# A forgetting-attention and latent-attention layer: decays ahead of the first head, early weight blocks split tile by tile, and copies and small subtractions given to GpSimd

## The chip, the cores and the metric

The kernel runs on one core of a Trainium2 chip. The metric is the device time of one execution in microseconds. Before the change the median of three runs is 655.59 us (654.94 to 655.67).

## The reference

One layer of an encoder: 1024 frames and 16 meta tokens in front of them, model width 1024. One input projection feeds two groups of eight heads. The FoX heads are causal softmax attention with a forgetting bias, the MLA heads are chunk-causal attention on low-rank latents. Both are gated by a SiLU, joined, projected, normed and added to the input.

```python
h = _rmsnorm(x, norm_pre)
proj = h @ w_in
(fq, fk, fv, f_logit, f_gate, c_q, c_kv, k_r, m_gate) = jnp.split(proj, ...)
log_f = jax.nn.log_sigmoid((f_logit + b_f).astype(jnp.float32))
cum = jnp.cumsum(log_f, axis=1).transpose(0, 2, 1)
# FoX: s = q k / 8 + cum[query] - cum[key], key <= query, softmax, times fv
# MLA: q from c_q, k and v from c_kv, rope on 32 of 96 columns, mask by chunks of 64
y = jnp.concatenate([fox, mla], axis=-1) @ w_out
return x + _rmsnorm(y, norm_post)
```

## The kernel before

Nearly every product is made of float16 pairs: an operand is split into a high and a low part, and three products (high by high, high by low, low by high) are summed in PSUM. Scales that keep the pairs in range come from sums of squares.

**Projection stage (0 to about 137 us).** A loop at L583 goes over token tiles of 128 rows. For tile t it norms and transposes tile t + 1 (`norm`, `turn`; the cast to `xBh` or `xAh` is in `split`, L142), makes the latents and the forget logits (`latents`), the FoX values (`values`) and the MLA values (`latents_V`). Between these, weight blocks for the later stages are loaded to staging buffers with the tag "wr2" (`load_block(..., True)`, four buffers). Four early blocks (`raws_e`) are split to pairs by `block_parts` (L149 on ACT, L150 on DVE) when t is 5. Twelve late blocks are loaded three at a time when t is 5 to 8; each is only squared and summed (`square_block`, L465 on ACT), for its scale. `scale_blocks` turns the sums to scales. Behind the loop, `lu` (L644) is the log of the forget gates.

**Decays.** `decays` (L961) transposes `lu` (L969), copies it to `zt` (L971, L975), sums it along the frames (L976), takes its size (L979, L980, L982, a product cm at L984) and derives from it the factors of the FoX operands, `fox_c` (L997), `fox_qc` and `fox_inv`; it scales `ncum` (L986, L987) and cuts it into three float16 parts (`cparts`, L1005 to L1008), which go through DRAM into rows 64 to 66 of the operand K2 (L1041). It is called from the job of head 0, behind the products of its first chunk.

**FoX heads (about 158 to 400 us).** `fox_proj(h)` makes the operands of head h in three chunks of columns (512, 264, 264): `chan_group` has 24 products (L955 to L957) into one of two PSUM buffers, then ACT copies queries to QS[0:64] and Q2[0:64] (L1047, L1048) and keys to KS[0:64] and KS[64:128] (L1049, L1050), and DVE writes the low parts QS[64:128] and K2[0:64] (L1053, L1054), after which the PSUM buffer is free. The work of head h + 1 and of the gates runs in slices between the four steps of head h.

**A step** (`step`, L873) takes two query tiles: scores on PE (L793, L796), maxima on DVE (L803, L804, L808), exponentials on ACT to `pr` (L816), high parts on ACT to `ph` (L829). One step later DVE writes the low parts (L833) and the low parts of the 16 meta columns (L898), and SP issues a transposing DMA of `ph` to `pT` (L901). Three steps after the scores PE multiplies with the values (L841, L842) and DVE sums the result (L913). `pr` has two buffers, `ph` three (filled with zeros once, L771), `pT` three. MLA heads run the same steps from about 400 to 600 us; the output projection follows.

The program builder takes the source order as a priority and places an instruction on its engine by when its inputs should be there, so that the order on an engine is not that of the source.

## Time and profile before

| | us |
|---|---|
| median of the runs | 655.59 |
| profiled execution, its own time | 651.95 |
| its span, first to last instruction | 650.2 |
| PE busy in the span | 562.1 |
| DVE busy | 501.2 |
| ACT busy | 421.4 |
| GpSimd (POOL) busy | 148.7 |

The profiled execution is one run of the program; its own time is a little under the median of the runs. Busy times are unions over the span, and those of PE are modelled ends of pipelined matmuls. An idle time in brackets is that of the engine just before the instruction, with the instruction or DMA whose end released it; where several were waited for, it names the one that came last by the profile. PEclk is the share of 2.4 GHz that TensorE was granted.

### The profile page before, as it was taken

The page shows a single profiled execution, that of the slowest core. Times are in us where ns is not written, and L with a number is a line of the kernel's source. Part 1 is how long each engine was busy: PE and PEld are TensorE (multiplying, and loading weights), DVE is VectorE, ACT ScalarE, POOL GpSimd, SP SyncE. Part 2 cuts the span into 40 slices and gives each one's busy share as a digit, 9 for nine tenths or more (in the row PEclk, how much of TensorE's full clock was granted, in tenths as well). Part 3 has the DMA queues.
Part 4 walks back from the last instruction along what each step waited for, and adds up shares of the span by engine and source line. Part 5 has one row for each costly group of instructions (what it writes and reads, how often), then busy time and mean ns, then how long its engine had stood idle before and what let it go on. Part 6 is the DMA issues. An engine that isn't in the chain of part 4 may idle for free.

```text
span 650.2 us, 11363 instructions
## 1 busy us (share of the span) xinstructions
PE 562.1 (86%) x4100; PEld 362.4 (56%) x4100; DVE 501.2 (77%) x1048; ACT 421.4 (65%) x855; POOL 148.7 (23%) x179
## 2 busy tenths in 40 slices
PE   1999598992899999899999986978989989987994
PEld 1445254551556565656566543555756756666784
DVE  4787965458677978787887988779998887995667
ACT  6686757643777686767687737567866776646332
POOL 2233333274000101010010331003102202262462
PEclk9999798995999999999999988998999999999998
DMA  9945569935175968495969667599999799799963
GB/s 305 231 118 127 113 121 241 225 85 150 42 152 124 187 133 174 105 222 111 231 115 204 143 157 145 112 229 218 162 227 178 164 211 187 158 227 211 313 233 122
DMA packets 277944, 112.36 MB, mean 173 GB/s; under 512 B 235312, under 2 KB 265008, under 8 KB 277888
## 3 DMA queue, kind: packets, MB, share of 16 engines
q1 hardware_dynamic: 277888, 111.64, 76.1%
q8 instruction: 32, 0.52, 0.3%
q14 instruction: 24, 0.20, 0.1%
HBM read 52.05 MB, written 17.63 MB: 107 GB/s over the span
## 4 chain that ended last, share of the span: by engine, by line
DVE 33%; PE 30%; ACT 19%; DMA 8%; issue 7%; POOL 1%; SPq 0%; DVEq 0%; ACTq 0%; POOLq 0%
ACT pr L816 8%; DVE ph L833 7%; DVE nb L803 5%; ACT ph L829 4%; PE s L793 4%; DMA pT<-ph 3%; DVE nb L804 3%; PE psg L955 2%; DMA wr<-in_w_in 2%; PE psg L956 2%; PE psg L957 2%; PE avs L842 2%; DVE nbs L808 2%; DVE st L1054 1%; PE psf L1251 1%
## 5 line engine op out<-in xcount | busy, mean ns | idle before, releaser
L833 DVE TENSOR_TENSOR ph<-pr,ph 128x896 f16<-128x896 f32 (+7 forms) x128 | 104.2, 822 | 38.2 <-ACT ph L829 37.5
L816 ACT ACTIVATE pr<-s,nbs,fox_inv 128x144 f32<-128x144 f32 (+8 forms) x72 | 56.1, 784 | 56.3 <-DVE nbs L808 54.0
L793 PE MATMUL s<-st,st 128*128 128x348 f16 (+6 forms) x434 | 77.3, 307 | 14.5 <-DVE st L1053 8.2
L816 ACT ACTIVATE pr<-s,nbs,ism 128x144 f32<-128x144 f32 (+8 forms) x72 | 56.1, 785 | 42.6 <-DVE nbs L808 19.1
L842 PE MATMUL avs<-Vt,pT 128*128 128x128 f16 x704 | 69.7, 222 | 12.9 <-DMA pT<-ph 6.6
L793 PEld LDWEIGHTS <-st 128*128 128x128 f16 x560 | 50.9, 98 | 48.8 <-issue 14.2
L829 ACT CAST ph<-pr 128x912 f16<-128x912 f32 (+6 forms) x112 | 77.6, 737 | 0.3
L803 DVE TENSOR_REDUCE nb<-s 128x1 f32<-128x344 f32 (+4 forms) x80 | 68.2, 857 | 7.6 <-PE s L796 6.5
L842 PEld LDWEIGHTS <-pT 128*128 128x128 f16 x704 | 59.3, 99 | 14.7 <-DMA pT<-ph 12.9
L841 PE MATMUL avs<-Vt,pT 128*128 128x64 f16 x576 | 61.7, 194 | 0.0
L841 PEld LDWEIGHTS <-pT 128*128 128x128 f16 x576 | 51.1, 99 | 4.3 <-issue 3.7
L955 PEld LDWEIGHTS <-wp 128*128 128x128 f16 x320 | 31.8, 99 | 34.5 <-DVE st L1054 11.2
L850 POOL TENSOR_TENSOR onat<-onat,rs 128x512 f32<-128x512 f32 x8 | 8.8, 1103 | 164.4 <-DVE onat L913 141.3
L956 PEld LDWEIGHTS <-wp 128*128 128x128 f16 x320 | 31.7, 99 | 26.3 <-issue 5.6
L957 PEld LDWEIGHTS <-wp 128*128 128x128 f16 x320 | 31.8, 99 | 25.8 <-issue 1.7
L955 PE MATMUL psq<-xAh,wp 128*128 128x264 f16 x128 | 36.2, 283 | 3.0 <-DVE st L1054 2.6
L956 PE MATMUL psq<-xAl,wp 128*128 128x264 f16 x128 | 36.1, 282 | 0.0
L957 PE MATMUL psq<-xAh,wp 128*128 128x264 f16 x128 | 36.1, 282 | 0.0
L804 DVE TENSOR_REDUCE nb<-s 128x1 f32<-128x144 f32 (+1 forms) x64 | 31.9, 498 | 3.6 <-PE s L796 3.2
L145 POOL TENSOR_TENSOR ogl<-ogr,ogh 128x512 fp32r<-128x512 f32 (+1 forms) x16 | 19.8, 1238 | 46.8 <-ACT ogh L142 46.8
L955 PE MATMUL psg<-xAh,wp 128*128 128x512 f16 x64 | 24.3, 380 | 7.1 <-DVE st L1054 7.1
L145 POOL TENSOR_TENSOR st<-qt,st 128x512 f16<-128x512 f32 x8 | 10.2, 1274 | 81.2 <-ACT st L142 81.2
(367 smaller groups left out, 1574.3 us busy)
## 6 DMA issues: line engine op xcount, KB each, us to landing
wr<-in_w_in SPq DMA_DIRECT2D x20, 512.0 KB, 5.4
wr<-in_w_in SPq DMA_DIRECT2D x26, 256.0 KB, 3.9
wor<-in_w_out SPq DMA_DIRECT2D x8, 512.0 KB, 4.9
xt<-in_x SPq DMA_DIRECT2D x7, 512.0 KB, 5.1
og_d<-og SPq DMA_DIRECT2D x14, 256.0 KB
y_d<-ys SPq DMA_DIRECT2D x12, 256.0 KB, 2.2
y<-y_d SPq DMA_DIRECT2D x6, 512.0 KB
xr<-in_x SPq DMA_DIRECT2D x6, 512.0 KB, 4.8
```

The costliest lines, as they stand in the source:

```text
L145: lo_eng.tensor_tensor(lo, raw, hi.bitcast(F32) if hi.dtype == F32R else hi, ALU.subtract)
L793: T.matmul(o, sta[:, i * P : (i + 1) * P], mov[:, k0 : k0 + w], start=q == 0, stop=q == len(passes) - 1 and not last)
L803: V.tensor_reduce(nb[:, k : k + 1], part, AX.X, ALU.max, negate=True)
L804: V.tensor_reduce(nb[:, 1:2], parts_b[0], AX.X, ALU.max, negate=True)
L816: A.activation(pr[:, c0:c1], part, AF.Exp, bias=nb, scale=inv, accum_out=sums[:, c : c + 1])
L829: A.copy(ph[:, 112 : 112 + W], pr)
L833: V.tensor_tensor(lo, pr[:, NM:W], ph[:, P : P + W - NM], ALU.subtract)
L841: T.matmul(avf[:, 0:HD], lo[:, j - 1, :], Vt[:, j, vh, 0], start=False, stop=False)
L842: T.matmul(avf, hi[:, j, :], Vt[:, j, vh].rearrange("p t d -> p (t d)"), start=j == 0, stop=j == n)
L955: T.matmul(ps[:, 0:n], hi[:, c, :], xT(0, c, c0, n), start=c == 0, stop=False)
L956: T.matmul(ps[:, 0:n], hi[:, c, :], xT(1, c, c0, n), start=False, stop=False)
L957: T.matmul(ps[:, 0:n], lo[:, c, :], xT(0, c, c0, n), start=False, stop=c == NC - 1)
```

## The change

It has five parts. The staging tag "wr2" gets a fifth buffer. Each early block is split in its own tile, t = 4 to 7, and the twelve late blocks are loaded in tiles 5 to 7 (3, 4 and 5). The zeroing of `ph` covers the 96 columns of two blocks that nothing else writes. `decays` is called before the job of head 0, and in it the scaling of `ncum` comes behind `fox_inv`. In FoX, Q2[0:64] and KS[64:128] are copied by GpSimd from QS[0:64] and KS[0:64], where ACT read PSUM a second time. The low parts of the meta columns (L898) are made by GpSimd, in all 64 steps.

```diff
--- before.py
+++ after.py
@@ -244,7 +244,7 @@
     def load_w(k, cols):
 
         pl, tag = ((fw, "wr"), (xa, "wr2"))[k % 2]
-        raw = pl.tile([P, 2, 512], F32, name="wraw", tag=tag, bufs=3 if k % 2 == 0 else 4)
+        raw = pl.tile([P, 2, 512], F32, name="wraw", tag=tag, bufs=3 if k % 2 == 0 else 5)
         o = 0
         for c0, n in cols:
             SY.dma_start(raw[:, :, o : o + n], wv[:, 2 * (k % 4) : 2 * (k % 4) + 2, c0 : c0 + n],
@@ -451,7 +451,7 @@
     def load_block(block, staged=False):
         kind, k = block
         segs = {"q": ((COL_FQ + k * HD, HD), (COL_FK + k * HD, HD)), "f": ((COL_FG + k * P, P),), "m": ((COL_MG + k * P, P),)}[kind]
-        pl, tag, bufs = (xa, "wr2", 4) if staged else (fw, "wr", 3)
+        pl, tag, bufs = (xa, "wr2", 5) if staged else (fw, "wr", 3)
         raw = pl.tile([P, NC, P], F32, name="wr", tag=tag, bufs=bufs)
         o = 0
         for c0, n in segs:
@@ -599,13 +599,13 @@
         for b, raw in raws_l:
             square_block(b, raw)
         raws_l = []
+        if t < NT:
+            b, raw = raws_e[t - 4]
+            early[b] = block_parts(b, raw)
+            if t > 4:
+                raws_l = [(b, load_block(b, True)) for b in [late_blocks.popleft() for _ in range((3, 4, 5)[t - 5])]]
         if t == 5:
-            for b, raw in raws_e:
-                early[b] = block_parts(b, raw)
             wkr0 = load_ukv(0)
-        if t >= 5:
-            raws_l = [(late_blocks.popleft(), None) for _ in range(3)]
-            raws_l = [(b, load_block(b, True)) for b, _ in raws_l]
         if t == 6:
             sums = xa.tile([P, 4], BF16, name="usums")
             for c in range(2):
@@ -625,8 +625,6 @@
             turn(t + 1)
 
 
-    for b, raw in raws_l:
-        square_block(b, raw)
     latents_T(NT)
     z = xa.tile(FN, F32, name="z")
     V.tensor_tensor(z, fnat, bf.unsqueeze(1).to_broadcast(FN), ALU.add)
@@ -768,7 +766,7 @@
     NPH = 3
     phs = [at.tile([P, NBLK * P], F16, name=f"ph{k}", tag=f"ph{k}", bufs=1) for k in range(NPH)]
     for ph in phs:
-        G.memset(ph, 0.0)
+        G.memset(ph.rearrange("p (b k) -> p b k", k=P)[:, 0 : NT + 3 : NT + 2, 0:96], 0.0)
 
     WT = 344
 
@@ -895,7 +893,7 @@
                 low(i, p, h, l)
             ph, n1 = prev["ph"].rearrange("p (b k) -> p b k", k=P), prev["prw"].rearrange("p (b k) -> p b k", k=NM)
             w0 = 1 + 8 * (prev["t"][0] + 1)
-            V.tensor_tensor(ph[:, 0 : B0 + 1 : B0, 96:112], n1[:, 0 : w0 + 1 : w0, :],
+            G.tensor_tensor(ph[:, 0 : B0 + 1 : B0, 96:112], n1[:, 0 : w0 + 1 : w0, :],
                             ph[:, 0 : B0 + 1 : B0, 112:128], ALU.subtract)
             prev["pT"] = at.tile([P, NBLK * P], F16, name="pT", tag="pT", bufs=3).rearrange("p (b k) -> p b k", k=P)
             SY.dma_start_transpose(prev["pT"], prev["ph"])
@@ -983,9 +981,6 @@
         cm = ps_s.tile([P, 2, 512], F32, name="cm", tag="s2")[:, 0, 0:H]
         T.matmul(cm, ones8, dg, start=True, stop=True)
 
-        V.tensor_scalar(cmh[:, 1:2].bitcast(I32), cmh[:, 0:1].bitcast(I32), -1.0, float(268 << 23), ALU.mult, ALU.add)
-        V.tensor_scalar(ncum, ncum, cmh[:, 1:2], None, ALU.mult)
-
 
         e = at.tile([P, 5, H], F32, name="fe", tag="fe")
         cme, emax, ie, ex, cmx = (e[:, k, :] for k in range(5))
@@ -999,6 +994,9 @@
         V.tensor_tensor(fox_qc, cmx, ex, ALU.mult)
         V.reciprocal(ie, ex)
         V.scalar_tensor_tensor(fox_inv, ie, 0.125, ie, ALU.mult, ALU.mult)
+
+        V.tensor_scalar(cmh[:, 1:2].bitcast(I32), cmh[:, 0:1].bitcast(I32), -1.0, float(268 << 23), ALU.mult, ALU.add)
+        V.tensor_scalar(ncum, ncum, cmh[:, 1:2], None, ALU.mult)
         cparts = []
         for k in range(NCUM):
             cparts.append(at.tile([P, NBLK * P], F16, name=f"cp{k}", tag="pT", bufs=3)[0:H, 0:L])
@@ -1035,8 +1033,6 @@
                 ps = product("psq")
                 yield from chan_group(ps, w, c0, n)
                 if k == 0:
-                    if h == 0:
-                        decays()
                     G.tensor_copy(Q2[64 : 64 + n3, 0:S], fox_qc[64 : 64 + n3, h : h + 1].to_broadcast([n3, S]))
                     SY.dma_start(K2[64 : 64 + n3, :], cum_d[:, h, :])
                 q0 = max(c0, NM)
@@ -1045,13 +1041,13 @@
                 pk = ps[64:128, 0:n]
                 ks = slice(c0, c0 + n)
                 A.activation(QS[0:64, qs], pq, AF.Copy, scale=cq)
-                A.activation(Q2[0:64, qs], pq, AF.Copy, scale=cq)
                 A.activation(KS[0:64, ks], pk, AF.Copy, scale=ckk)
-                A.activation(KS[64:128, ks], pk, AF.Copy, scale=ckk)
+                G.tensor_copy(Q2[0:64, qs], QS[0:64, qs])
+                G.tensor_copy(KS[64:128, ks], KS[0:64, ks])
 
                 def evac(pq=pq, pk=pk, qs=qs, ks=ks):
                     V.scalar_tensor_tensor(QS[64:128, qs], pq, cq, QS[0:64, qs], ALU.mult, ALU.subtract)
-                    V.scalar_tensor_tensor(K2[0:64, ks], pk, ckk, KS[64:128, ks], ALU.mult, ALU.subtract)
+                    V.scalar_tensor_tensor(K2[0:64, ks], pk, ckk, KS[0:64, ks], ALU.mult, ALU.subtract)
                 evacuate_later(evac)
                 yield n / 400.0
         return 10.4, gen(), load_w(("q", h), w)
@@ -1095,6 +1091,7 @@
         for g in GATES[h]:
             add_job(h, *gate_job(*g))
 
+    decays()
     add_job(-1, *fox_proj(0))
     fox_jobs(0)
     work(-1, 3.0)
```

## Rows read from the trace of the kernel before

**Rows 1.** Windows: stretch, length, busy PE, PEld, DVE, ACT, POOL, clock, DMA share, GB/s

```profile
74.00:84.30 10.30, 6.10 (x17) 2.49 (x18) 8.98 (x18) 7.12 (x13) 5.19 (x9) 0.50 0.72 146
149.20:162.80 13.60, 4.03 (x18) 2.61 (x19) 10.54 (x24) 5.08 (x10) 4.02 (x3) 0.50 0.41 110
164.00:347.00 183.00, 174.20 (x1394) 109.78 (x1392) 146.42 (x272) 135.00 (x256) 12.31 (x11) 1.00 0.73 147
430.00:600.00 170.00, 148.18 (x1267) 107.59 (x1264) 145.18 (x298) 116.70 (x244) 41.10 (x28) 0.98 0.93 198
```

**Rows 2.** Timeline of PE: start, duration, instruction, [idle before, releaser]

```profile
75.96 0.53 PE L304 MATMUL ps<-w1h,xBh 128*128 128x424 f16 x1 [4.68 <-ACT xBh L142]
79.09 0.90 PE L420 MATMUL pl<-ident,nt 128*128 128x128 f32 x3 [2.23 <-DVE nt L397]
...
150.25 0.16 PE L984 MATMUL cm<-dg,ones 8*128 8x8 bf16 x1 [3.49 <-POOL ph L771]
158.62 0.47 PE L793 MATMUL s<-st,st 128*128 128x344 f16 x1 [8.20 <-DVE st L1053]
```

**Rows 3.** timeline of all engines from 136 to 160 us, the decays

```profile
136.38 0.23 DVE L644 SCALAR_TENSOR_TENSOR lu<-z,lu 128x72 f32<-128x72 f32 x1
...
137.15 0.38 PE L969 MATMUL pf<-ident,lu 128*8 128x128 f32 x2
...
142.70 0.82 PE L969 MATMUL pf<-ident,lu 128*8 128x128 f32 x6
...
143.44 0.16 ACT L971 COPY zt<-pf 8x16 f32<-8x16 f32 x1 [4.67 <-DMA vm_d<-vm]
...
143.56 6.58 POOL L771 MEMSET ph<- 128x2560 f16 x3 [0.63 <-DMA wqr<-in_w_uq]
...
144.69 2.31 DVE L976 TENSOR_TENSOR_SCAN ncum<-ones8f,zt 8x1040 f32<-8x1040 f32 x1 [6.57 <-ACT zt L975]
...
147.66 2.49 DVE L982 TENSOR_SCALAR dg<-ident,cmh 8x8 bf16<-8x8 f32 x1
...
154.89 0.21 DVE L997 SCALAR_TENSOR_TENSOR fox_c<-fe,isx,bisc 128x8 f32<-128x8 f32 x1
...
155.14 0.68 ACT L1047 ACTIVATE st<-psq,fox_c 64x512 f16<-64x512 f32 x1 [9.36 <-DVE fox_c L997]
...
158.59 0.75 DVE L1054 SCALAR_TENSOR_TENSOR st<-psq,fox_c,st 64x512 f16<-64x512 f32 x1
```

**Rows 4.** timeline, the early blocks at 70 us; ACT later in the projection

```profile
70.79 1.28 DVE L150 SCALAR_TENSOR_TENSOR wp<-wr,bsc,wp 128x1024 f16<-128x1024 f32 x1
70.85 2.17 ACT L149 ACTIVATE wp<-wr,bsc 128x1024 f16<-128x1024 f32 x2
...
75.32 1.07 ACT L142 CAST xBh<-pt 128x512 f16<-128x512 f32 x2
...
104.46 1.06 ACT L465 ACTIVATE junkb<-wr 128x1024 bf16<-128x1024 f32 x1 [2.50 <-DMA wr<-in_w_in]
```

**Rows 5.** groups of ACT from 164 to 347 us: count, busy us, mean ns, idle before

```profile
L1050 ACT ACTIVATE st<-psq,fox_c 64x264 f16<-64x264 f32 (+1 forms) x19 | 10.3, 541 | 0.2
```

**Rows 6.** who PE waited for: us in total, times, longest us

```profile
PE psg L955 <- DVE st L1054: 7.1, 5, 1.6
```

**Rows 7.** timeline of DVE before PE's wait at 211 us

```profile
209.12 0.97 DVE L803 TENSOR_REDUCE nb<-s 128x1 f32<-128x784 f32 x1
...
210.10 0.47 DVE L1053 SCALAR_TENSOR_TENSOR st<-psq,fox_c,st 64x248 f16<-64x248 f32 x1
```

**Rows 8.** groups of DVE: count, busy us, mean ns, idle before

```profile
L898 DVE TENSOR_TENSOR ph<-pr,ph 128x32 f16<-128x32 f32 x64 | 18.4, 287 | 0.1
```

**Rows 9.** timeline, POOL and DVE at 247.5 us

```profile
247.54 1.08 POOL L1040 CAST st<-fox_qc 3x1024 f16<-3x1024 f32 x1 [2.24 <-PE s L796]
...
247.64 1.01 DVE L898 TENSOR_TENSOR ph<-pr,ph 128x32 f16<-128x32 f32 x1
```

**Rows 10.** groups of POOL by form: count, busy us, mean ns, idle before

```profile
L402 POOL TENSOR_TENSOR t<-kr,rnat 128x32 f32<-128x32 f32 x9 | 3.4, 376 | 53.1 <-DVE kr L400 53.1
```

## The prediction, made before the changed kernel was seen

> **What bounds the kernel now.** I read the busy shares by stretch first, then the places where PE idles and who ended that idling, then the instructions around the two worst of them. TensorE sets the pace: it is busy 174.2 of 183.0 us in the FoX heads and 148.2 of 170.0 us in the MLA heads, where DVE with 145.2 us is nearly as full [rows 1]. So time is won where PE waits. Two places stand out. Near 76 us, in the projection stage, PE waits 4.68 us and then 2.23 us, and the whole stretch 74.0 to 84.3 runs at a granted clock of 0.50, that is 1.2 instead of 2.4 GHz [rows 1, 2]. Between the projection and head 0 it waits 3.49 and 8.20 us, with only the 0.16 us product cm between, and the clock falls to 0.50 again until 162.8 us [rows 1, 2]. The rest is small: 7.1 us in five waits for L1054 in FoX [rows 6], scattered waits in MLA.
>
> The instructions of an engine do not stand in the order of the source: two of the transposes of `decays` (L969) ran at 137.15 us, ahead of the first product of the job that calls it, six at 142.70 behind it [rows 3]. A moved line therefore changes a priority, and only shifts what was not put there anyway.
>
> **Part 1, decays first, small memsets, half of the ACT copies at head 0.** `lu` is done at 136.61 (136.38 + 0.23), yet the bulk of the transposes comes 6 us later; ACT had nothing to do for the 4.67 us before 143.44 [rows 3]. From there the chain is serial: copies 1.25 us (143.44 to 144.69), scan 2.31, two small steps 0.66, dg 2.49, then 4.85 us from cm at 150.25 to the end of `fox_c` at 155.10, because DVE does pieces of `ncum` and `cparts` in between [rows 2, 3]. dg is an 8x8 operation and ends at 150.15, within 0.01 us of the end of the memsets (143.56 + 6.58 = 150.14); an operation as small as L997 takes 0.21 us [rows 3]. So the large memsets cost 2.3 us here. With `decays` ahead: nine transposes at 0.14 us (six took 0.82) from 137.15 to 138.4, ACT free at 138.77, copies until 140.0, scan until 142.3, small steps until 143.0, dg until 143.2, and the same 4.85 us to `fox_c` at 148.1 instead of 155.10. I keep the 4.85 us: `ncum` now stands behind `fox_inv` in the source, but L1005 and L1008 stood there before and were put into the chain all the same. That is 7.0 us.
>
> Behind `fox_c`, the first chunk took 4.20 us to leave its PSUM buffer (L1047 at 155.14 to the end of L1054 at 159.34): four ACT copies of 0.68 us one after the other and then two DVE operations of 0.75 us [rows 3]. With two ACT copies, and L1053 beside the second of them, L1054 ends 0.68 + 0.68 + 0.75 = 2.1 us after the start, which gives another 2.1 us. PE goes on at about 150.2 instead of 159.34, 9.1 us earlier. At the lower clock PE did 4.03 us of work between 149.2 and 162.8 [rows 1], 2.0 us of which come back if the shorter idle time (146.8 to 150.2) does not bring the clock down; I take 0.9. Sum: 10.0 us. Bounds: at least 2.3 + 2.1 = 4.4 us if nothing moves, at most 159.34 - 146.8 + 2.0 = 14.5 us, since the first two chunks keep PE busy until 146.8 (150.25 - 3.49) [rows 2]. The low end needs the 4.67 us that ACT idled to stay unused, so I stay above the middle. The three stores of `cparts` and the load of K2's rows on SP move with the chain; scores need them only in their second pass, behind the third chunk, so I cost them at nothing; if chunk 3 no longer covers them, what shows is part of the 4.85 us that DVE spends on `cparts` and the chain.
>
> **Part 2, early blocks one per tile, five staging buffers.** At 70 us four splits come in a row; two ACT halves take 2.17 us, a DVE half 1.28 us, and the cast of `xBh`, for which PE waits, comes at 75.32 [rows 2, 4]. The scale of the blocks exists only just before, so the first two splits (tiles 4 and 5) stay at this place and two go to tiles 6 and 7. That takes 2.2 us from ACT and 2.6 us from DVE ahead of PE: the wait of 4.68 us falls to 2.5, that of 2.23 us to about nothing, together 4.4 us, and part of the 3.05 us that 6.10 us of work lost at the low clock [rows 1]; I take 1.0 of it. The two splits moved cost what ACT and DVE had free there, which I put at nothing while PE is the slower; if that cover is gone they cost 2.4 us each on DVE or ACT. The twelve late blocks are now loaded in three tiles (3, 4, 5) instead of four (3 each), on the same SP queue as the x tiles and stores; ACT waited 2.50 us for such a block at 104.46 [rows 4], and its casts stand behind that. For this I take 0.4 off. Sum: 5.0 us, between 0 and 9.9 (4.68 + 2.23 + 3.05).
>
> **Part 3, second places copied by GpSimd.** In FoX ACT loses two of four copies per chunk, 0.54 us each [rows 5]. What PE waits for is L1054 on DVE, and in the repeated case at 211 us DVE came to L1053 straight from L803 with no idle time [rows 7]: a faster ACT alone does not move it. Of the 7.1 us [rows 6] I take 1.5; the bounds are 0 and 7.1. The copies themselves: no copy of this shape is in the trace; a cast of 1024 columns took 1.08 us [rows 9], so 512 columns take 0.54 and 250 to 264 take 0.27, 2.2 us per head and 17.6 us in all. Only the scores of the next head need them, and the projection that makes them ends while the present head still runs, so I let PE wait for none. But GpSimd holds up DVE: L898, whose mean is 0.29 us, took 1.01 us and ended with the cast beside it [rows 8, 9]. If all 17.6 us fell on a DVE that PE waits for, they would cost 17.6 us; PE-bound FoX hides nearly all, I take 0.5 loss. The Trainium skill ("SBUF — State Buffer", Who interferes with whom) says that a DVE instruction with two SBUF inputs contends with a GpSimd instruction that reads SBUF, and that the second one blocks fully; the pair at 247.54 agrees. By the same page an instruction that only writes blocks merely the two-port modes, and the memset beside the scan and dg fits: the scan ran, dg waited.
>
> **Part 4, meta low parts to GpSimd.** DVE loses 64 operations, 18.4 us [rows 8]. On GpSimd a subtraction of 128x32 took 0.38 us [rows 10], 24.1 us for 64. Its inputs are there as soon as the low parts can start, so it runs beside L833, which also reads twice from SBUF, and may hold it up as long. The transposing DMA then waits for GpSimd and DVE; queued behind a GpSimd operation, it comes later, with three steps of slack. Half of either lies in MLA: at best 9.2 us gained there, at worst 12.0 - 9.2 = 2.8 us lost; PE waits in only part of the steps, so I take 0.5 gain.
>
> **Sum.** 10.0 + 5.0 + 1.5 - 0.5 + 0.5 = 16.5 us. The profiled execution took 651.95 us around a span of 650.2 us; that gives 635.45. The median of the runs, 655.59, is 3.64 above it, so 639.1, rounded to 639.0.
>
> **The rivals.** Moved lines land where they were: only the memset's 2.3 us, 2.1 us of shorter evacuation and 1.0 us elsewhere remain, 650.2 us. For it: two transposes were already early [rows 3]. Against: the other seven were not, and ACT stood idle.
>
> Loads too dense: each of the three tiles in which ACT waits for late blocks adds some 2.5 us of it [rows 4], which eats part 2: 644.1 us. For it speaks DMA 0.72 busy near 74 us [rows 1], against it that the fifth buffer lets the first load start earlier.
>
> All waits go: 14.5 + 9.9 + 4, 627.2 us.
>
> The lock on the other side: copies and metas hold DVE up in full, 17.6 + 24.1 - 18.4 = 23.3 us, against 15.0 us from parts 1 and 2: 663.9 us. It decides once more than 65% of the 23.3 us lies in front of PE. For it: the 1.01 us pair, and DVE 85% busy in MLA; against it: FoX is PE-bound [rows 1], and the 18.4 us that DVE gives up stand in it already. The Trainium skill ("Perfetto Trace Analysis", Optimizing Scalar/DVE Operations) warns that moving work between these two engines might not help for this reason; no run here has shown it yet for such small operations.
>
> **How the numbers follow.** Forecast (630 to 648) 50%, moved lines stay 13%, dense loads 15%, all waits go 15%, lock 7%. The range 625 to 650 leaves out the lock, half of the first rival and a part of the third. Faster by over 0.2% (1.3 us, about what a measurement of this kernel can tell from no change): 91%; within: 3%; slower: 6%.
>
> **What would show it.** Right: all L969 before the first L955 of head 0, the scan starting near 140 us after the same `lu`, dg near 0.2 us, PE's idle time before head 0 at 3 to 5 us instead of 11.7, the two waits near 76 us under 3 us together, and FoX and MLA as long as before within 3 us. Wrong: if L969 still runs behind the first chunk, if ACT waits for `wr` loads behind 100 us, or if L833's mean in MLA rises by more than 0.1 us and the heads become longer.

## The result, and the profile of the changed kernel

The changed kernel takes 636.52 us in the median of 4 runs (636.23 to 638.45), the kernel before beside it 655.27: a ratio of 0.972, 95% interval 0.970 to 0.974. In a later set of runs the two took 635.06 and 655.27, ratio 0.970 (0.967 to 0.973). The forecast was 639.0, range 625 to 650. The profiled execution took 636.23 us around a span of 634.4; its granted clock is 0.977 in the mean, before 0.964.

The lines of the changed kernel carry numbers two to five lower: L967 to L974 are the transposes, the copies into `zt` and the scan (before L969 to L976), L980 is dg (before L982), L992 `fox_c` (before L997), L791 the scores (before L793). L1036 is GpSimd's cast of `fox_qc`, L1043 and L1044 are ScalarE's copies, L1045 and L1046 GpSimd's, L1049 and L1050 the low parts (before L1053 and L1054), L896 the meta low parts (before L898). ACT is ScalarE, DVE VectorE, POOL GpSimd, PE TensorE.

I cut the two spans at six events that both traces have; head 7 ends with its last reduction, at 422.3 us before and at 406.9 after. The numbers are differences of start and end times, in us:

| stretch | before | after | gain |
|---|---|---|---|
| start to the first matmul | 9.93 | 11.06 | -1.13 |
| first matmul to `lu` | 126.68 | 118.09 | 8.59 |
| `lu` to the end of `fox_c` | 18.49 | 17.01 | 1.48 |
| `fox_c` to the first score | 3.52 | 3.90 | -0.38 |
| first score to the end of head 7 (FoX) | 263.66 | 256.86 | 6.80 |
| heads 8 to 15 (MLA) | 186.85 | 186.30 | 0.55 |
| rest | 41.06 | 41.23 | -0.17 |

So nearly everything came from the first stage and the FoX heads, and the decays (third and fourth row), on which most of the forecast rested, gave 1.1 us. The first row is no effect: in the profiles of all runs here the first matmul starts between 9.4 and 11.1 us, in two of the changed kernel itself at 11.06 and 10.57.

The windows of the changed kernel that answer to the first two of [rows 1] (stretch, length, busy time of PE, PEld, DVE, ACT, POOL, clock, DMA share, GB/s):

```profile
76.40:79.90 3.50, 3.50 (x12) 1.57 (x10) 3.46 (x10) 3.47 (x10) 1.28 (x7) 0.51 0.71 148
144.70:155.00 10.30, 4.94 (x23) 3.38 (x24) 6.30 (x16) 3.00 (x6) 5.22 (x6) 0.50 0.51 126
```

The half-clock stretch near 76 us has shrunk from 10.2 us to 3.4, the one around the first score from 13.7 to 10.2. PE's waits that answer to [rows 2], on its timeline (start, duration, instruction, idle before it and releaser):

```profile
73.66 0.35 PE L304 MATMUL ps<-w1h,xBh 128*128 128x424 f16 x1 [2.33 <-ACT xBh L142]
76.08 0.35 PE L306 MATMUL ps<-w1h,xBl 128*128 128x424 f16 x1 [1.89 <-DVE xBl L145]
...
141.28 0.16 PE L982 MATMUL cm<-dg,ones 8*128 8x8 bf16 x1 [1.34 <-issue]
...
150.06 0.45 PE L791 MATMUL s<-st,st 128*128 128x344 f16 x1 [7.94 <-POOL st L1046]
```

The 4.68 us have become 2.33, the 2.23 us 1.89 and the 3.49 us 1.34, but the wait for the first score is 7.94 us where it was 8.20, and GpSimd's copy of KS now ends it. The decays between, on the timeline of all engines, to be laid beside [rows 3]:

```profile
128.92 0.23 DVE L642 SCALAR_TENSOR_TENSOR lu<-z,lu 128x72 f32<-128x72 f32 x1
...
130.46 1.04 PE L967 MATMUL pf<-ident,lu 128*8 128x128 f32 x8
...
131.46 0.62 ACT L351 CAST vm<-vs 128x512 f16<-128x512 f32 x1
...
133.16 1.16 POOL L352 TENSOR_TENSOR vm<-vs,vm 128x512 f16<-128x512 f32 x1
...
134.34 0.36 SPq L438 DMA_DIRECT2D vm_d<-vm  x1
...
136.74 0.16 ACT L969 COPY zt<-pf 8x16 f32<-8x16 f32 x1 [4.66 <-DMA vm_d<-vm]
...
136.86 0.66 POOL L769 MEMSET ph<- 128x192 f16 x3 [0.63 <-DMA wqr<-in_w_uq]
...
137.99 2.31 DVE L974 TENSOR_TENSOR_SCAN ncum<-ones8f,zt 8x1040 f32<-8x1040 f32 x1 [6.57 <-DMA wqr<-in_w_uq]
...
140.97 0.22 DVE L980 TENSOR_SCALAR dg<-ident,cmh 8x8 bf16<-8x8 f32 x1
```

Eight of nine transposes are done by 131.5 us, much as forecast. But ACT, free at 132.08, begins the copies only at 136.74, 7.59 us after the end of `lu` (129.15); before it was 6.83 (143.44 - 136.61). The wait that ends with the store of `vm` is there in both kernels: 4.67 us in [rows 3], 4.66 here, where the store lands at 136.64 us.

### The profile page after: what moved, and what is told of

Same layout as the page of the kernel before. It is cut to its first block, busy times and chain, and to the rows that moved or that the text cites. A ratio compares the mean times of both kernels' runs of the same rounds, so it can differ in the third digit from the quotient of the medians.

```text
span 634.4 us, 11456 instructions
## 1 busy us (share of the span) xinstructions
PE 555.5 (88%) x4100; PEld 361.3 (57%) x4100; DVE 485.2 (76%) x984; ACT 397.2 (63%) x807; POOL 217.0 (34%) x291
## 4 chain that ended last, share of the span: by engine, by line
PE 37%; DVE 27%; ACT 15%; DMA 10%; issue 8%; POOL 1%; SPq 1%; DVEq 0%; ACTq 0%; POOLq 0%
ACT pr L814 7%; DVE ph L831 5%; DVE nb L801 4%; PE s L791 4%; ACT ph L827 4%; DMA pT<-ph 4%; PE psg L953 3%; PE psg L954 3%; PE psg L955 3%; DMA wr<-in_w_in 3%; PE avs L840 2%; DVE nb L802 2%; PE psq L953 2%; PE psf L1247 2%; PE psf L1246 2%
## 5 line engine op out<-in xcount | busy, mean ns | idle before, releaser
L831 DVE TENSOR_TENSOR ph<-pr,ph 128x128 f16<-128x128 f32 (+7 forms) x128 | 109.4, 863 | 38.6 <-ACT ph L827 37.2
L896 POOL TENSOR_TENSOR ph<-pr,ph 128x32 f16<-128x32 f32 x64 | 48.3, 755 | 203.3 <-ACT ph L827 106.7
L791 PE MATMUL s<-st,st 128*128 128x348 f16 (+6 forms) x434 | 77.4, 308 | 16.0 <-POOL st L1046 8.2
L791 PEld LDWEIGHTS <-st 128*128 128x128 f16 x560 | 51.0, 98 | 49.6 <-issue 14.4
L801 DVE TENSOR_REDUCE nb<-s 128x1 f32<-128x344 f32 (+4 forms) x80 | 68.2, 857 | 11.4 <-PE s L794 8.2
L150 DVE SCALAR_TENSOR_TENSOR wp<-wr,bsc,wp 128x1024 f16<-128x1024 f32 x21 | 28.2, 1342 | 0.0
L953 PE MATMUL psg<-xBh,wp 128*128 128x512 f16 x64 | 25.0, 391 | 2.9 <-DVE og L859 2.2
```

What stands on the lines that cost most here:

```text
L791: T.matmul(o, sta[:, i * P : (i + 1) * P], mov[:, k0 : k0 + w], start=q == 0, stop=q == len(passes) - 1 and not last)
L801: V.tensor_reduce(nb[:, k : k + 1], part, AX.X, ALU.max, negate=True)
L831: V.tensor_tensor(lo, pr[:, NM:W], ph[:, P : P + W - NM], ALU.subtract)
L896: G.tensor_tensor(ph[:, 0 : B0 + 1 : B0, 96:112], n1[:, 0 : w0 + 1 : w0, :], ph[:, 0 : B0 + 1 : B0, 112:128], ALU.subtract)
L953: T.matmul(ps[:, 0:n], hi[:, c, :], xT(0, c, c0, n), start=c == 0, stop=False)
```

## The experiments

Each is the changed kernel with one edit, unless it says otherwise. Ratios are to the kernel before, run beside it; the changed kernel's are 0.972 and 0.970. The runs came in three sets, in which the median of the kernel before was 654.51, 655.66 and 655.27 us, so I read nothing into 1 us between sets. Lengths of stretches come from one profiled execution of each kernel.

### The decays: order of the calls, or a wait on a store

The memory map of the built program suggests why the store is the releaser. A pool is a region of memory from which tiles are taken; when it is closed, a later pool may be laid over it. `zt` and `ncum` are tiles of the pool `at`, which covers part of the closed pool `xs`. The reading to be tested is that whoever first writes a tile of `at` waits for everything still outstanding on all of `xs`. Its last user is the store of `vm`, though `vm` itself lies above the end of `at` and `zt` shares no byte with `xs`. One run takes the reason of the wait away, one puts the order of the calls back.

```
+    xv, xv_st = pool("xv", side="right")
     xs, xs_st = pool("xs", bufs=2, side="right")
...
-        lat = xs.tile([P, 2, 4, P], F16, name="lat", tag="lat", bufs=3)
+        lat = xv.tile([P, 2, 4, P], F16, name="lat", tag="lat", bufs=3)
...
-        vm = xs.tile([P, H, 2, HD], F16, name="vm", tag="vm", bufs=1)
+        vm = xv.tile([P, H, 2, HD], F16, name="vm", tag="vm", bufs=1)
...
     xs_st.close()
+    xv_st.close()
```

> The changed kernel with one move: the tiles lat and vm, which stores to HBM read late, get a pool of their own that lies above the memory of the pool at. The memory map, the tiles and every instruction stay the same. Theory A (in the decays the copies into zt, the first tiles of the pool at, wait for everything that was still outstanding on the closed pool xs below it, last of all the store of vm, and that is the 4.66 us of ScalarE before the copies at 136.74 us in the profile of the changed kernel): the copies begin within 0.5 us of the end of the last Vt/vm cast at 132.08, fox_c comes 4 to 5 us earlier, and the time is 3.5 to 5.5 us below the changed kernel's 636.5, 631 to 633. Rival B (ScalarE had nothing else to do there, as my prediction read the row of before; the copies are late for another reason, or the chain after fox_c takes up the gain): the time stays within 1 us of 636.5.

Measured: 634.47 us, ratio 0.968 (0.965 to 0.972). Its timeline (line numbers are one or two higher here):

```profile
130.65 0.23 DVE L643 SCALAR_TENSOR_TENSOR lu<-z,lu 128x72 f32<-128x72 f32 x1
133.06 0.16 ACT L971 COPY zt<-pf 8x16 f32<-8x16 f32 x1
...
134.78 2.32 DVE L976 TENSOR_TENSOR_SCAN ncum<-ones8f,zt 8x1040 f32<-8x1040 f32 x1 [1.63 <-ACT zt L975]
...
143.55 0.21 DVE L994 SCALAR_TENSOR_TENSOR fox_c<-fe,isx,bisc 128x8 f32<-128x8 f32 x1
...
147.25 0.47 PE L793 MATMUL s<-st,st 128*128 128x344 f16 x1 [3.98 <-DVE st L1051]
```

The copies come 2.2 us after `lu` and not 7.6, with no wait before them, and ahead of the last store of `vm`, which is issued only at 138.07. The memsets of `ph`, tiles of `at` too, now run at 126.61, before `lu`. `fox_c` ends 12.87 us after `lu` (17.01 in the changed kernel), the first score starts 16.37 after it (20.91), and PE's wait for it is 3.98 us (7.94). So the wait is theory A's, and in the changed kernel it held the first score up by 4.5 us. The time fits neither theory: the median fell by 2.0 us against the first set of the changed kernel and by 0.6 against the later one. At the end of head 0, 3.4 of the 4.5 us are left (70.4 us after `lu`, 73.8 in the changed kernel); in the profiled execution, the slowest of the four, the first stage then took 119.92 us with 6.8 us at half clock (118.09 with 3.4) and the MLA heads 187.15 (186.30).

```
                 if k == 0:
+                    if h == 0:
+                        decays()
...
-    decays()
     add_job(-1, *fox_proj(0))
```

> The changed kernel with the call of decays() put back to where it was, inside the projection of head 0 (the reordered lines inside decays and all other parts of the change stay). Theory A (the order was never what made the copies late, the wait on the store of vm was): the time rises by no more than 2 us, to 636 to 638.5. Rival B (my prediction: the copies were late because they came behind the projection): it rises by about 7 us, to 643.5.

Measured: 635.50 us, ratio 0.970 (0.967 to 0.973): no change, theory A. Its timeline shows that even with six transposes behind the first chunk again the copies begin behind the same wait:

```profile
128.00 0.23 DVE L642 SCALAR_TENSOR_TENSOR lu<-z,lu 128x72 f32<-128x72 f32 x1
...
135.09 0.82 PE L967 MATMUL pf<-ident,lu 128*8 128x128 f32 x6
...
135.82 0.16 ACT L969 COPY zt<-pf 8x16 f32<-8x16 f32 x1 [4.67 <-DMA vm_d<-vm]
```

`lu` to the end of `fox_c` takes 17.01 us in both. In the decays ACT, DVE and POOL run the same instructions in the same order with the call at either place; only PE's order changes.

This shows that the order is worth nothing while the wait stands, and no more than that. The six transposes run from 6.9 to 7.7 us after the end of `lu` here, and the copies start 7.6 after it: the order alone would have held all but the first of the copies up to nearly the same moment as the store. So in the kernel before two hold-ups of almost equal length stood side by side ([rows 3]: transposes from 142.70, copies at 143.44), and the 4.5 us of the run with the pool are those of taking away both. Taking away the late order alone brought nothing. Taking away the wait alone, with the call at its old place, was not run; from these rows I estimate a gain of about 0.3 us.

### The memsets

```
-        G.memset(ph.rearrange("p (b k) -> p b k", k=P)[:, 0 : NT + 3 : NT + 2, 0:96], 0.0)
+        G.memset(ph, 0.0)
```

> The changed kernel with the three memsets of the whole ph tiles again. Theory A (my prediction: dg was held to 2.49 us until the third memset ended, and that stands on the path to fox_c): dg takes about 2 us again where the memsets lie beside it, fox_c comes 1.5 to 2.5 us later after lu, the time rises by 1.5 to 2.5 us, to 637.5 to 639. Rival B (the wait on the store of vm now puts the memsets beside the copies into zt and the scan, and what they hold up there is the scan alone, or nothing, since the next wait behind fox_c, for GpSimd's copies, takes it up): within 0.7 us of 636.

Measured: 636.95 us, ratio 0.973 (0.969 to 0.977). The hold-up of dg is back exactly as in [rows 3]:

```profile
136.58 6.58 POOL L769 MEMSET ph<- 128x2560 f16 x3 [0.62 <-DMA wqr<-in_w_uq]
...
140.70 2.49 DVE L980 TENSOR_SCALAR dg<-ident,cmh 8x8 bf16<-8x8 f32 x1
143.28 0.16 PE L982 MATMUL cm<-dg,ones 8*128 8x8 bf16 x1 [3.61 <-POOL ph L769]
```

`fox_c` ends 19.23 us after `lu`, 2.22 later than in the changed kernel: theory A's size. In the time only 0.4 to 1.9 us of it show, less than theory A's range for it. Head 0 ends 2.8 us later after `lu`, and heads 1 to 7 then take 202.3 us and not 204.0: the half-clock stretch of 3.4 us that lies at 387 us in head 7 of the changed kernel lies at 366 us here. Whether that 1.6 us belongs to the later start or to chance stays open.

### The first stage: the split, or the fifth buffer

Part 2 is two edits: the split of the early blocks, with the loads of late blocks that go with it, and the fifth buffer of the staging ring. Three runs take them apart: the split alone put back, the ring alone put back, and the kernel before with nothing but the ring.

```
-        if t < NT:
-            b, raw = raws_e[t - 4]
-            early[b] = block_parts(b, raw)
...
         if t == 5:
+            for b, raw in raws_e:
+                early[b] = block_parts(b, raw)
...
+            raws_l = [(late_blocks.popleft(), None) for _ in range(3)]
...
```

> The changed kernel with the early blocks split all at token tile 5 again and the late blocks loaded three a tile, the last three squared behind the loop (the ring keeps its five buffers). Theory A (the split one a tile is the whole of the 7.5 us by which the first stage ends earlier, lu at 129.15 and not at 136.61): the time rises by 6.5 to 8.5 us, to 643 to 645, and the half-clock stretch of 10 us near 74 us is back. Rival B (my prediction: worth 5.0 us; the rest came with the fifth buffer, which stays here, or with the run): it rises by 4 to 5.5 us, to 640.5 to 642.

Measured: 637.57 us, ratio 0.972 (0.968 to 0.977): 1 to 2.5 us above the changed kernel, and both theories missed. First matmul to `lu` took 119.41 us.

```
-        raw = pl.tile([P, 2, 512], F32, name="wraw", tag=tag, bufs=3 if k % 2 == 0 else 5)
+        raw = pl.tile([P, 2, 512], F32, name="wraw", tag=tag, bufs=3 if k % 2 == 0 else 4)
...
-        pl, tag, bufs = (xa, "wr2", 5) if staged else (fw, "wr", 3)
+        pl, tag, bufs = (xa, "wr2", 4) if staged else (fw, "wr", 3)
```

> The changed kernel with the staging ring at four buffers, as before; the split one a tile and the loads of 3, 4 and 5 late blocks stay. With the split put back and five buffers kept, lu ended at 130.24 us, 6.4 us earlier than before and only 1.1 later than with the whole change. Theory A (most of the gain of the first stage is the fifth buffer's: it lets the loads of late blocks be issued while the early ones still stand in the ring, so that ScalarE squares late blocks from 55 us on and the queue behind those loads moves up): here lu ends at 133 to 136 us and the time rises by 4 to 6 us, to 639.5 to 642. Rival B (either one alone brings most of it: the two parts mend the same wait, TensorE's 4.68 us before 75.96 in the kernel before): lu ends by 131 and the time stays within 2 us of 636.

Measured: 641.79 us, ratio 0.981 (0.976 to 0.985), `lu` at 134.25 us: theory A in both. The reverse of that diff, applied to the kernel before:

> The kernel before with nothing but a fifth buffer in the staging ring. Theory A (in the first stage the fifth buffer is nearly the whole gain: with it and the old split, lu came 119.4 us after the first matmul, with both 118.1, with the split alone 124.9, before 126.7): here lu comes 119 to 120.5 us after the first matmul and the time is 5 to 7.5 us below before, 648 to 650.5. Rival B (the decays and head 0 take up part of it, or the early end needs the other loads of the change): 651 to 655.

Measured: 646.87 us, ratio 0.988 (0.985 to 0.991), first matmul to `lu` 119.63 us: theory A in the stage, and a time still below its range. Against the profiled execution of before the gain is 5.2 us, against the medians 8.4. So of the 8.59 us of this stage the fifth buffer alone brings 7.05 (126.68 to 119.63), the split alone 1.78 (to 124.90). Two executions of one program differ by up to 1.5 us in this stage (last section), so the 1.78 are hardly clear of that, and the 7.05 are. PE's wait shows the same, with the split and four buffers and then with the old split and five:

```profile
74.22 0.35 PE L304 MATMUL ps<-w1h,xBh 128*128 128x424 f16 x1 [4.68 <-ACT xBh L142]
```

```profile
73.78 0.50 PE L304 MATMUL ps<-w1h,xBh 128*128 128x424 f16 x1 [2.25 <-ACT xBh L142]
```

What the buffer does is seen on ACT and DVE of the kernel before with five buffers:

```profile
55.15 1.06 ACT L465 ACTIVATE junkb<-wr 128x1024 bf16<-128x1024 f32 x1
...
60.94 1.06 ACT L465 ACTIVATE junkb<-wr 128x1024 bf16<-128x1024 f32 x1 [2.31 <-DMA wr<-in_w_in]
...
67.01 0.17 DVE L161 TENSOR_SCALAR bsc<-mb 128x4 int32<-128x4 int32 x1
...
67.33 1.28 DVE L328 SCALAR_TENSOR_TENSOR xt<-xt,rx,gB 128x1024 f32<-128x1024 f32 x1
67.41 1.15 ACT L149 ACTIVATE wp<-wr,bsc 128x1024 f16<-128x1024 f32 x1
```

Two late blocks are loaded early enough to be squared (L465) at 55 and 61 us, where ACT has room; in the kernel before the first late square comes at 76.33. And the order on DVE has changed: the scale of the blocks (L161) stands ahead of the normalisation of an x tile (L328), where before it stood behind it:

```profile
68.01 1.28 DVE L328 SCALAR_TENSOR_TENSOR xt<-xt,rx,gB 128x1024 f32<-128x1024 f32 x1
...
69.40 0.17 DVE L161 TENSOR_SCALAR bsc<-mb 128x4 int32<-128x4 int32 x1
...
69.61 1.15 ACT L149 ACTIVATE wp<-wr,bsc 128x1024 f16<-128x1024 f32 x1 [1.80 <-DVE bsc L161]
```

So ACT's first split starts 2.2 us earlier without a wait, and with it all that follows up to the cast of `xBh`, with the four splits still in one row. Which of the two, earlier squares or the order on DVE, is worth how much was not separated.

### FoX: two copies and a subtraction on GpSimd

```
-                G.tensor_copy(Q2[0:64, qs], QS[0:64, qs])
-                G.tensor_copy(KS[64:128, ks], KS[0:64, ks])
+                A.activation(Q2[0:64, qs], pq, AF.Copy, scale=cq)
+                A.activation(KS[64:128, ks], pk, AF.Copy, scale=ckk)
```

> The changed kernel with the second places of the FoX operands (Q2 rows 0-63, KS rows 64-127) written by ScalarE from PSUM again and not copied by GpSimd. Theory A (the growth of the gain through the FoX heads, from 10.7 us at the end of head 0 to 15.4 us at the end of head 7, is this part's: 0.67 us a head): the time rises by 4 to 6 us, to 640.5 to 642.5; the PE waits in heads 1 to 7 grow by as much. Rival B (my prediction: worth 1.0 us in all, and the growth comes from the other parts through the order of the work): it rises by 0.5 to 1.5 us, to 637 to 638; through the faster first evacuation at head 0, where the changed kernel waits for GpSimd's copy of KS until 150.06 us, it could even fall by 1 us.

Measured: 640.30 us, ratio 0.978 (0.975 to 0.981): theory A, 0.2 us below its range.

```
-            G.tensor_tensor(ph[:, 0 : B0 + 1 : B0, 96:112], n1[:, 0 : w0 + 1 : w0, :],
+            V.tensor_tensor(ph[:, 0 : B0 + 1 : B0, 96:112], n1[:, 0 : w0 + 1 : w0, :],
```

> The changed kernel with the low parts of the meta keys (64 subtractions 128x2x16) on VectorE again. Theory A (VectorE is not the bound of a step, and GpSimd's 64 subtractions, 755 ns in the mean, run beside the long low parts and put off nobody): the time stays within 1.5 us of 636, and the ends of the MLA heads relative to head 7 stay within 1 us. Rival B (the 18.4 us of VectorE that this part freed are worth a quarter or more, 0.07 us a step and more): the time rises by 4 us or more, to 640.

Measured: 640.81 us, ratio 0.979 (0.975 to 0.984): theory B. But not in MLA, which took 185.39 us; the loss lies in FoX. Each edit alone thus cost about 5 us there, out of 6.8 that the whole gained, and the next run put back both:

> The changed kernel with both GpSimd parts of the FoX heads put back: ScalarE writes the second places, VectorE the meta low parts. Each of them put back alone cost 4 to 5 us, and in the profiles the stretch from the first score to the end of head 7 went from 256.4 us to 261.5 and to 261.4, against 263.3 in the kernel before. Theory A (the two relieve one and the same wait, TensorE's for the last low part of an operand, in which ScalarE's copies and VectorE's queue stand one behind the other; with one of them back the other is worth only 1.8 us): the stretch takes 262.5 to 264 us and the time is 641.5 to 643.5, 5.5 to 7 above the changed kernel. Rival B (the two are separate gains that add): the stretch takes 266 us or more, the time is 645 or more.

Measured: 646.57 us, ratio 0.987 (0.985 to 0.990). First score to the end of head 7 (here, as in the first table, up to the end of the last reduction):

| meta low parts | second places | us | PE's wait psg <- L1050 |
|---|---|---|---|
| GpSimd | GpSimd | 256.86 | 3.9 |
| GpSimd | ScalarE | 261.88 | 6.9 |
| VectorE | GpSimd | 261.85 | 6.9 |
| VectorE | ScalarE | 265.07 | 7.0 |

Neither theory holds as it stood: the first edit brings 3.2 us, whichever it is, the second 5.0, together 8.2. Measured as in the expectation, to the start of the last reduction, the stretch is 264.7 us, between the two theories and nearer to A; the time is in the range of B, since the MLA heads are 2.8 us longer than in the changed kernel run beside it (188.51 against 185.67). There four half-clock stretches of 3.4 us fell where the other has one; why, stays open. The wait in the last column is that of [rows 6], in the view of whom PE waited for, here of the changed kernel, then with ScalarE's copies, then with the meta parts on VectorE, then with both (us in total, times, longest):

```profile
PE psg L953 <- DVE st L1050: 3.9, 5, 1.3
```

```profile
PE psg L953 <- DVE st L1050: 6.9, 5, 1.5
```

```profile
PE psg L953 <- DVE st L1050: 6.9, 4, 1.8
```

```profile
PE psg L953 <- DVE st L1050: 7.0, 5, 1.5
```

This wait accounts for a part of it. Whichever edit comes second takes 3.0 of its 5.0 us from it. The 3.2 us of the first do not stand there (7.0 and 6.9). Over the stretch PE is not busy for 20.1 us with both put back, for 18.5 (ScalarE's copies) and 18.9 (meta parts on VectorE) with one, and for 13.8 with none. It is busy for 245.0 us with both put back and for 243.0 to 243.4 in the other three, and at half clock for 12.3 us against 8.3 to 8.7. So the second edit took away idle time alone; of the first edit's 3.2 us about half is idle time and half the shorter time at half clock.

What the two edits do to the wait is seen in one of its cases. With ScalarE's copies DVE takes a maximum of 0.97 us (L801) ahead of the low parts, although the KS that they read is written by 293.11 (L1044), before that maximum starts:

```profile
292.63 0.48 ACT L1044 ACTIVATE st<-psq,fox_c 64x264 f16<-64x264 f32 x1
...
293.30 0.97 DVE L801 TENSOR_REDUCE nb<-s 128x1 f32<-128x784 f32 x1
...
294.28 0.47 DVE L1049 SCALAR_TENSOR_TENSOR st<-psq,fox_c,st 64x248 f16<-64x248 f32 x1
...
294.76 0.50 DVE L1050 SCALAR_TENSOR_TENSOR st<-psq,fox_c,st 64x264 f16<-64x264 f32 x1
...
295.32 0.39 PE L953 MATMUL psg<-xAh,wp 128*128 128x512 f16 x1 [1.40 <-DVE st L1050]
```

So it is the order on DVE that holds PE up there. It is the same in all five such waits of that run, and in [rows 7]. In the other two, with the meta parts on VectorE and in the changed kernel, the low parts follow the long L831 at once, and the maximum comes behind them:

```profile
291.26 1.09 DVE L831 TENSOR_TENSOR ph<-pr,ph 128x896 f16<-128x896 f32 x1 [0.43 <-ACT ph L827]
...
292.37 0.47 DVE L1049 SCALAR_TENSOR_TENSOR st<-psq,fox_c,st 64x248 f16<-64x248 f32 x1
...
293.41 0.39 PE L953 MATMUL psg<-xAh,wp 128*128 128x512 f16 x1 [1.71 <-DVE st L1050]
```

```profile
288.07 1.09 DVE L831 TENSOR_TENSOR ph<-pr,ph 128x896 f16<-128x896 f32 x1 [0.43 <-ACT ph L827]
...
289.68 0.50 DVE L1050 SCALAR_TENSOR_TENSOR st<-psq,fox_c,st 64x264 f16<-64x264 f32 x1
...
290.21 0.97 DVE L801 TENSOR_REDUCE nb<-s 128x1 f32<-128x784 f32 x1
290.23 0.39 PE L953 MATMUL psg<-xAh,wp 128*128 128x512 f16 x1 [0.78 <-DVE st L1050]
```

But with the meta parts on VectorE PE's wait begins 0.4 us after that L831 has started (291.70), in the changed kernel 1.4 us after it (289.45): DVE is 0.9 us later against PE. GpSimd's copies go with the better order, GpSimd's subtractions with the earlier DVE. Where the rest of the second edit's 5.0 us lies, about 2 us, I did not work out.

### A version that is faster still

On top of the pool of its own, the cum parts leave VectorE, and GpSimd's copies go ahead of its cast:

```
-            V.tensor_copy(cparts[k], ncum)
+            A.copy(cparts[k], ncum)
...
-                V.tensor_tensor(ncum, ncum, cparts[k], ALU.subtract)
+                G.tensor_tensor(ncum, ncum, cparts[k], ALU.subtract)
...
-                    G.tensor_copy(Q2[64 : 64 + n3, 0:S], fox_qc[64 : 64 + n3, h : h + 1].to_broadcast([n3, S]))
...
                 G.tensor_copy(KS[64:128, ks], KS[0:64, ks])
+                if k == 0:
+                    G.tensor_copy(Q2[64 : 64 + n3, 0:S], fox_qc[64 : 64 + n3, h : h + 1].to_broadcast([n3, S]))
```

> The changed kernel with the pool of its own for lat and vm (which brought fox_c from 17.0 to 12.9 us after lu and the first score from 20.9 to 16.4 after it), and two more moves in the decays: the three casts of the cum parts on ScalarE, the two subtractions between them on GpSimd, so that the eight small VectorE steps from cm to fox_c (4.2 us there, 3.8 of it casts and subtractions put between them) run in one piece; and for each head GpSimd's two copies ahead of its cast of fox_qc into Q2. Theory A (that chain is what the first score waits for): fox_c comes 9 to 10 us after lu, the first score 13 to 14.5 us after lu, and the time falls by another 2 to 3 us against the run with the pool alone, to 631 to 633. Rival B (ScalarE's casts stand among its first evacuations, GpSimd's subtractions before the copies of the operands, and K2's load from HBM comes later, so that the score waits for these): fox_c is early, the first score stays 16 to 17 us after lu, and the time is 634 to 636.

> The version with the pool of its own for lat and vm, the cum parts' casts on ScalarE and subtractions on GpSimd, and GpSimd's copies ahead of its cast, in five rounds beside the changed kernel. If what its one profile showed (first end of head 0 at 198.3 us, 2.6 earlier than with the pool alone and 4.3 earlier than the changed kernel) is the kernel's and not that run's, it lies 3.5 to 5.5 us below the changed kernel on this chip, 631 to 633; if it was the run, within 2 us of it.

The changed kernel stood beside the second of these runs:

> The changed kernel as it is, beside the other runs of this chip, so that their differences from it can be read without another chip between them: 635.5 to 637.5 us.

Measured: 631.77 us, ratio 0.965 (0.960 to 0.970), and again 631.35, ratio 0.964 (0.961 to 0.967); the changed kernel beside the second 635.06, ratio 0.970 (0.967 to 0.973): 3.7 us. Its timeline in the second run:

```profile
128.59 0.23 DVE L643 SCALAR_TENSOR_TENSOR lu<-z,lu 128x72 f32<-128x72 f32 x1
...
138.34 0.23 DVE L994 SCALAR_TENSOR_TENSOR fox_c<-fe,isx,bisc 128x8 f32<-128x8 f32 x1
...
144.28 0.29 PE L955 MATMUL psq<-xAh,wp 128*128 128x264 f16 x1 [3.07 <-DVE st L1053]
```

`fox_c` ends 9.75 us after `lu` (17.01). The time is as expected, and the first score is not: it starts 19.84 us after `lu`, not 13 to 14.5: the third chunk's products now come ahead of it, so that start no longer marks the same event. The end of head 0 does: 67.9 us after `lu`, in the changed kernel 73.8, a gain of 5.9 us in two executions of each. Of these the pool alone gave 3.4; the other two edits were not taken apart. PE's long wait there is 3.07 us and the half-clock stretch 3.4 us (10.2). In the time 3.7 us remain: in the profiled execution the MLA heads took 187.54 us, in that of the changed kernel beside it 185.67; why, stays open.

## Why the prediction was right or wrong

**The sum was near by luck; its terms were not.** 16.5 us were forecast and 15.7 found between the profiled executions (18.8 between the medians). By term: part 1 gave 1.1 us and not 10.0, part 2 8.6 and not 5.0, parts 3 and 4 in FoX and MLA 7.4 and not 1.5. The errors cancelled. Of the signs that were to show the forecast right, dg came true (0.22 us) and, but for one, the transposes. The scan starts 8.8 us after `lu` and not 3.4, PE idles 9.3 us before head 0 and not 3 to 5, the two waits near 76 us make 4.2 us and not under 3, and FoX is 6.8 us shorter where it was to stay within 3.

**Part 1 failed at one reading:** "ACT had nothing to do for the 4.67 us before 143.44". The row itself names what ended that idle time, the DMA of `vm` [rows 3], and the prediction passes over it, as `zt` has no data from `vm`. The wait was not for data but for memory, and it held the copies up about as long as the late transposes did. So the 7.0 us of the moved chain, into which the memsets' 2.3 us were counted, became 1.5 us: the memsets' 2.2 us, measured, nothing for the order while that wait stood, also measured, less 0.8 us by which the copies came later after `lu` than before. The 4.85 us from cm to `fox_c` held (4.88). The rival that moved lines land where they were named the right outcome for this part and the wrong cause: eight transposes did move, to no effect.

**The 2.1 us behind `fox_c` failed at its last step.** From ACT's start to the first score took 3.8 us (146.25 to 150.06), before 3.5 (155.14 to 158.62). The last low part came earlier, but less than forecast: 3.10 us after ACT's start (149.35), before 4.20 (159.34), forecast 2.1. Nor was it what the first score had waited for, which began before it ended (158.62). And I let PE go on as soon as the low parts were written and said of GpSimd's copies: "Only the scores of the next head need them". At head 0 the score needs them at once, and before them stood the cast of `fox_qc`, which took 2.09 us here, and 1.08 in [rows 9].

**Part 2 had the right place and too small a size**, because I priced the split and took the fifth buffer for its servant. It is the other way round: 7.05 us the buffer alone, 1.8 the split. The wait of 4.68 us was to fall to 2.5 by the split and fell to 2.33, but that was luck: with the split alone it stays at 4.68, with the buffer alone it is 2.25. The other of the two waits, forecast at about nothing, is 1.89. The forecast of more waits on dense loads, a rival at 15%, did not come: ahead of the squares ACT waited 4.1 us for late blocks, in three waits, and 3.9 us in three before.

**Parts 3 and 4** were sized from the argument that a faster ACT does not move DVE where DVE is not idle [rows 7], and that a PE at 95% hides the rest. The first half failed: DVE was not idle, but what it did there was a maximum of 0.97 us, and in the changed kernel that stands behind the low parts. The second half failed for both edits, most for the two together: 3.2 us for the first alone, 8.2 for both. PE's wait of 7.1 us [rows 6] fell to 3.9; the rest came from its other waits and from less time at half clock. Part 3's 1.5 us lay inside its bounds, 0 to 7.1, and the value at the end I had not chosen. In part 4 the price of a subtraction on GpSimd was too small as well: 0.38 us forecast, 0.755 in the mean. **The lock** fell as a rival: low parts (L831) take 904 ns in the mean in MLA, before 839, 0.07 us more and under the 0.1 I had named as the sign, and the MLA heads did not become longer; it is mostly GpSimd that waits (below).

**The 3.64 us** between the profiled execution and the median, which I took to be constant, were the spread of the kernel before: its runs went from 651.8 to 658.0 us, and the profiled one was among the lowest. The changed kernel's profile lies 0.3 us under its median.

## What to carry to other kernels

The releaser in a row of idle time is evidence even when no data flows from it: ask whose memory the waiting tile takes, and keep tiles that late stores read out of the pools that the next stage's pool is laid over. When an edit changes nothing, look for a second hold-up of the same length before you call its reason wrong: here the late order of the calls and the wait on the store stood side by side. Take a part that is two edits apart before you price it; here one buffer more was worth about four times the reordering that it was to serve. Where two engines feed one wait, price the edits to them together: here the second brought 5.0 us and the first 3.2.

## What the runs showed of the hardware that I had not expected

A subtraction of 128x32 takes 183 ns in the median on VectorE (meta parts there) and 829 on GpSimd, which can do it in 243, because 49 of the 64 run beside a low part of VectorE's; the 15 that do not take 243 to 246:

```profile
L896 POOL TENSOR_TENSOR ph<-pr,ph x64: 243/829/1298, 164.2 to 578.6; 128x32 f16<-128x32 f32 x64
```

```profile
197.61 1.09 DVE L831 TENSOR_TENSOR ph<-pr,ph 128x896 f16<-128x896 f32 x1 [0.43 <-ACT ph L827]
197.71 1.09 POOL L896 TENSOR_TENSOR ph<-pr,ph 128x32 f16<-128x32 f32 x1 [5.93 <-ACT ph L827]
```

GpSimd starts 0.10 us after VectorE and ends 0.10 after it. The Trainium skill ("SBUF — State Buffer", Who interferes with whom) says that the instruction that was issued first keeps the shared ports and the other blocks; this pair agrees. So it is mostly GpSimd that pays, but not alone. In the MLA heads VectorE's low parts (L831) take 888 ns in the mean, and 819 with the meta parts on VectorE; over the 60 recorded ones that is 4.1 us, half of the 7.9 us that VectorE gave up there. Accordingly the MLA heads gained nothing from this move (186.30 us, 185.39 with the meta parts on VectorE). In FoX no such loss shows (840 and 860 ns).

The two long half-clock stretches lie at the long waits of PE near 75 us and before the first score, and grew shorter with these waits: 10.2 to 3.4 us and 13.7 to 10.2, in the fastest version 3.4 at the second place. Over the whole span the half-clock stretches add up to 47 us in the kernel before, 29 in the changed one and 17 in the fastest version. Not all of it goes by the waits: their number and length differ between executions of one program. Near 75 us the fastest version had 6.8 us of it in one and 3.4 in the other, and its first stage took 119.72 and 118.23 us; the changed kernel had 29 us in one execution and 25 in another. I therefore trust a stretch of a single profile to 1 or 2 us.
